# A decoder layer on one core: two of a summed pair's four weight sums made by accumulating DMAs, and three summed pairs per gate/up block in place of two

## The chip, the cores and the metric

The kernel runs on one core of a Trainium2 chip. The metric is the time of one execution on the device, in microseconds. The kernel before was timed three times: 1112.45, 1113.87 and 1114.35 us, median 1113.87 us. One more execution was profiled; it took 1112.63 us, and the trace below is of that one.

## The reference, cut to what matters

One layer of a hybrid decoder, for 256 tokens of width 2048, all in float32: a combined input projection, an RG-LRU branch and a retention branch, an output projection, and then the feed-forward part, which the change is about:

```
u  = rmsnorm(h, ln2_w)
ff = silu(u @ w_ffn_gate) * (u @ w_ffn_up)     # both weights (2048, 5632)
h  = h + ff @ w_ffn_down                       # weight (5632, 2048)
out = rmsnorm(h, final_norm_w)
```

Every weight is used once, so all of them come from DRAM during the run (the trace shows 211.67 MB read).

## The kernel before, in words

**Split products.** A float32 operand x is split into a high part h, rounded to the format that TensorE multiplies fast, and the remainder l = x - h. `split` (L100) does it: a cast on ScalarE (L101, the tiles `wh`, `bh`, `ah`), then a subtraction on VectorE (L102, the tiles `wl`, `bl`, `al`). A product of two such operands is three matmuls: high by high (L658), high by low of the weight (L659) and low by high (L660). All weights pass through this split while TensorE works, so ScalarE and VectorE have one cast and one subtraction for every 512 KB of weights.

**Feed-forward blocks.** The gate/up part has 11 blocks (`ffn_block`, L674), the down part 2 (`down_block`, L747). A block walks over pairs of 128-row slices of the contraction, 8 pairs in a gate/up block and 22 in a down block. A pair's weights are 1 MB, four pieces of 128 x 512, in the order b11, b12, b22, b21 along a row; the activations are likewise four pieces a11, a12, a21, a22 (class `Left`, L515). A plain pair is the 2 by 2 block product with eight products (`EIGHT`, L627), so 24 matmuls, and adds to four accumulators c11, c12, c21, c22. A **summed pair** uses seven products (`SEVEN`, L631), so 21 matmuls, of sums of pieces, and adds to the four c and to p1, p5, p6, p7, which are folded in after the last summed pair of the block. Its weight sums are

```
t1 = b11 + b12    t2 = t1 + b22    t3 = b12 + b22    t4 = t2 + b21
```

Before, pairs 2 and 4 of each gate/up block are summed (`SUMMED`, L32), and pairs 2, 6, 10, 14, 18 of each down block (`SUMMED_DOWN`, L33): 22 + 10 = 32 summed pairs. In this text S2 is the summed pair 2 of a block, Q3 the plain pair 3.

**Loading.** `Quad.load` (L603) is called for each half (512 KB) of a pair, three halves ahead of the pair that is computed (`AHEAD`, L933). A half goes by one DMA on SyncE's queue (SP) to a tile `raw` of 128 x 1024. There are five such tiles (`rpool`, L44), which the sum tiles also use, and four each of `wh` and `wl` (`wpool`, L45). For a plain pair each half is cut (split) where it lies, and its `raw` tile is free after the subtraction L102. For a summed pair b11 is split by itself into two activation tiles; when the second half is there, VectorE makes t1, t2 (into the tile `ta`) and t3, t4 (into `tb`), at L619, L620, L622, L623, and three cuts follow: (t1, t2), (t3, t4), (b22, b21). So a summed pair has 3.5 casts and 3.5 subtractions of 128 x 1024, a plain one 2 of each.

**Order.** The kernel is written step by step, and a scheduler then orders the instructions of each engine; each engine and each DMA queue takes its own in that order. PSUM has four banks `mm` (p1, p5, p6, p7, and the transposes `ft`, `ht` and `rms`) and four banks `aux` for c11 to c22. When a block's accumulators are done, VectorE adds them up (L720, L722), which frees their banks for the next block, ScalarE and VectorE make the gated result (L696 to L698), and TensorE transposes it (`turn`, L700) one and two steps later.

Of the kernel before, what the change touches and what calls it, by code (L numbers as in the profile page):

```python
# [28 lines left out]

SUMMED = (2, 4)  # L32
SUMMED_DOWN = (2, 6, 10, 14, 18)  # L33


# [1 line left out]
def tile_hymba_layer(ctx: ExitStack, tc: tile.TileContext, A: dict, out: bass.AP):  # L37
# [62 lines left out]
    def split(dst_h, dst_l, src):  # L100
        act.copy(out=dst_h, in_=src)  # L101
        v.tensor_tensor(out=dst_l, in0=src, in1=dst_h.bitcast(F32), op=ALU.subtract)  # L102
# [116 lines left out]
    def defer(steps, f):  # L219
        later.append([steps, f])  # L220
# [368 lines left out]
    class Quad:  # L589
# [11 lines left out]
                self.parts[name] = h[:, n * 512 : n * 512 + 512], l[:, n * 512 : n * 512 + 512]  # L601

        def load(self, half):  # L603
            r = rpool.tile([P, 1024], F32, tag="raw", name=nm("raw"))
            nc.sync.dma_start(out=r, in_=self.src[:, half * 1024 : half * 1024 + 1024])
            if half == 0 and self.before:
                self.before()
            if not self.sums:
                self.cut(("b22", "b21") if half else ("b11", "b12"), r)
                return  # L610
            if half == 0:
                self.ra = r
                self.parts["b11"] = act_tile("bh", F32R), act_tile("bl", F32R)
                split(*self.parts["b11"], r[:, :512])
                return
# [3 lines left out]
            v.tensor_tensor(out=t1, in0=b11, in1=b12, op=ALU.add)  # L619
            v.tensor_tensor(out=t2, in0=t1, in1=b22, op=ALU.add)  # L620
            self.cut(("t1", "t2"), ta)
            v.tensor_tensor(out=t3, in0=b12, in1=b22, op=ALU.add)  # L622
            v.tensor_tensor(out=t4, in0=t2, in1=b21, op=ALU.add)  # L623
            self.cut(("t3", "t4"), tb)
            self.cut(("b22", "b21"), r)

# [46 lines left out]

    def ffn_block(j):  # L674
        def after(i):
            if j == 0 and i == SUMMED[-1] + 1:
                norm2()
            if j in (1, 2) and i < 2:
                resid_tok(2 * j - 2 + i)
            if j == NB - 1 and i == 0:  # L680
                load_fw()

        ps = {}
        quads = [Quad(A["w_gu"][j * (KT // 2) + i], i in SUMMED) for i in range(KT // 2)]
        block(quads, hh, ffn_post(j, ps), ps, after=after)

    def ffn_post(j, ps):
        part = {}

        def other(c, name, a, b, op=ALU.subtract):  # L690
            part[c] = act_tile(name)
            v.tensor_tensor(out=part[c], in0=a, in1=b, op=op)

        def gated(t):
            g, u, th = part["c21" if t else "c11"], part["c22" if t else "c12"], act_tile("th")
            act.activation(out=th, in_=g, func=AF.Tanh, scale=r2_half[:, t : t + 1])  # L696
            v.scalar_tensor_tensor(out=g, in0=th, scalar=1.0, in1=g, op0=ALU.add, op1=ALU.mult)
            v.scalar_tensor_tensor(out=g, in0=u, scalar=r2_sq[:, t : t + 1], in1=g, op0=ALU.mult, op1=ALU.mult)  # L698

        def turn(b):  # L700
            pt = bank("ft")
            for c in range(2):
                for t, g in enumerate((part["c11"], part["c21"])):
                    o = c * S + t * P
                    pe.transpose(pt[:, o : o + P], g[:, (2 * b + c) * P : (2 * b + c) * P + P], ident)  # L705
# [24 lines left out]
        return post  # L730

# [316 lines left out]
```

## Time and profile before

| | |
|---|---|
| median of three executions | 1113.87 us (1112.45 to 1114.35) |
| profiled execution | 1112.63 us |
| its span, first to last instruction | 1110.9 us |
| gate/up blocks in it | about 387 to 862 us |
| down blocks in it | about 862 to 1100 us |
| read from DRAM | 211.67 MB, 192 GB/s over the span |

PE is TensorE, PEld its weight loads, DVE VectorE, ACT ScalarE, POOL GpSimd, SP SyncE, whose queue (SPq) issues nearly all loads. A row of a list of waits says which engine, at which line, waited for whom: microseconds in all, times, the longest. A row of a tile's list gives the duration in ns (least, median, most); its last line the time from a DMA's issue to its landing. A row of the timeline begins with the start and the length in microseconds; in brackets stands how long the engine was idle before, and who ended that. A row of stretches gives the busy time of each engine, the granted clock of TensorE, the busy share of the 16 DMA engines, and GB/s.

### The profile page before, as it was taken

Reading aid. Unit: us, or ns where it says so; the run is one execution under the profiler, and the core shown is the slowest. Engines: PE = TensorE matmul, PEld = TensorE weight load, DVE = VectorE, ACT = ScalarE, POOL = GpSimd, SP = SyncE. Lnnn points to the kernel's source line nnn. Section 1 sums busy time; section 2 is a strip of 40 time slices with the busy share of each in tenths; the row PEclk is TensorE's granted clock in tenths of the full one; section 3 lists DMA queues with packets and bytes.
Section 4 is the critical chain, followed back from the end, with each engine's and each line's share of the span. In section 5 each row is a group of like instructions: output and inputs, shape, how many; then the busy total and the mean of one; then the engine's idle time right before and its main releaser. Section 6 shows DMA issues by size and latency. Waiting matters only on the chain.

```text
span 1110.9 us, 15099 instructions
## 1 busy us (share of the span) xinstructions
PE 1096.1 (99%) x5584; PEld 934.2 (84%) x5584; DVE 878.0 (79%) x1229; ACT 617.3 (56%) x826; POOL 58.1 (5%) x64
## 2 busy tenths in 40 slices
PE   9999999999999999999999999999999999999995
PEld 7998888889988988888888888888888888888884
DVE  7797799978766787788778877877887988886665
ACT  7666644468465665554554555545546665554453
POOL 0602230000000000000000000000000000020001
PEclk9999999999999999999999999999999999999998
DMA  9764575554665555645746646656556456655662
GB/s 329 236 198 151 174 252 167 169 188 146 201 198 187 171 192 183 212 147 186 239 138 219 226 152 227 193 186 228 170 187 229 171 176 198 233 186 193 192 220 80
DMA packets 62218, 214.74 MB, mean 193 GB/s; under 512 B 7105, under 2 KB 7489, under 8 KB 62145
## 3 DMA queue, kind: packets, MB, share of 16 engines
q1 hardware_dynamic: 61344, 211.70, 57.8%
q0 software_dynamic: 512, 1.57, 0.4%
q8 instruction: 43, 0.70, 0.3%
q10 hardware_dynamic: 288, 0.52, 0.1%
q14 instruction: 31, 0.25, 0.1%
HBM read 211.67 MB, written 2.10 MB: 192 GB/s over the span
## 4 chain that ended last, share of the span: by engine, by line
PE 97%; ACT 1%; POOL 1%; DVE 0%; DMA 0%; issue 0%; SPq 0%; DVEq 0%; POOLq 0%
PE c L658 18%; PE c L659 18%; PE c L660 18%; PE fm L140 10%; PE fm L141 5%; PE fm L146 3%; PE fm L147 3%; PE fm L145 3%; PE p L660 3%; PE p L658 3%; PE p L659 3%; PE tm L156 3%; PE tm L157 3%; PE tm L158 3%; PE ft L705 1%; POOL sumsq L289 1%
## 5 line engine op out<-in xcount | busy, mean ns | idle before, releaser
L102 DVE TENSOR_TENSOR wl<-raw,wh 128x1024 fp32r<-128x1024 f32 (+1 forms) x368 | 440.7, 1209 | 151.2 <-ACT wh L101 149.4
L101 ACT CAST wh<-raw 128x1024 fp32r<-128x1024 f32 (+1 forms) x368 | 375.8, 1032 | 297.3 <-PE c L660 145.1
L659 PE MATMUL c<-wl,ah 128*128 128x512 f32 x864 | 333.1, 391 | 0.0
L660 PE MATMUL c<-wh,al 128*128 128x512 f32 x864 | 331.8, 389 | 0.0
L658 PE MATMUL c<-wh,ah 128*128 128x512 f32 x864 | 292.1, 389 | 0.0
L659 PEld LDWEIGHTS c<-wl,ah 128*128 128x128 f32 x864 | 162.2, 188 | 33.5 <-DVE wl L102 0.4
L658 PEld LDWEIGHTS c<-wh,ah 128*128 128x128 f32 x864 | 162.1, 188 | 33.4
L660 PEld LDWEIGHTS c<-wh,al 128*128 128x128 f32 x864 | 162.3, 188 | 33.0
L101 ACT CAST wh<-sum 128x1024 fp32r<-128x1024 f32 x64 | 66.8, 1054 | 81.3 <-PE c L660 52.7
L140 PE MATMUL fm<-u,wh 128*128 128x512 f32 x256 | 90.7, 398 | 0.0
L140 PE MATMUL fm<-y,wh 128*128 128x512 f32 x224 | 78.9, 398 | 0.0
L102 DVE TENSOR_TENSOR wl<-sum,wh 128x1024 fp32r<-128x1024 f32 x64 | 76.7, 1217 | 2.2 <-ACT wh L101 1.6
L146 PE MATMUL fm<-u,wh 128*128 128x256 f32 x256 | 72.7, 284 | 0.0
L145 PE MATMUL fm<-u,wh 128*128 128x256 f32 x256 | 72.7, 284 | 0.0
L147 PE MATMUL fm<-u,wl 128*128 128x256 f32 x256 | 72.3, 283 | 0.0
L141 PE MATMUL fm<-u,wl 128*128 128x256 f32 x256 | 71.9, 281 | 0.0
L141 PE MATMUL fm<-y,wl 128*128 128x256 f32 x224 | 62.4, 281 | 0.0
L807 POOL TENSOR_TENSOR htok<-htok,fw 128x512 f32<-128x512 f32 (+1 forms) x7 | 10.5, 1509 | 914.0 <-ACT junk L805 914.0
L140 PEld LDWEIGHTS fm<-u,wh 128*128 128x128 f32 x256 | 48.1, 188 | 11.7
L619 DVE TENSOR_TENSOR sum<-raw 128x512 f32<-128x512 f32 x32 | 22.0, 687 | 37.9 <-DMA raw<-in_w_down 23.0
L140 PEld LDWEIGHTS fm<-y,wh 128*128 128x128 f32 x224 | 41.9, 188 | 10.2
L146 PEld LDWEIGHTS fm<-u,wh 128*128 128x128 f32 x256 | 49.1, 192 | 0.1
(242 smaller groups left out, 1489.5 us busy)
## 6 DMA issues: line engine op xcount, KB each, us to landing
raw<-in_w_gu SPq DMA_DIRECT2D x176, 512.0 KB, 5.0
raw<-in_w_down SPq DMA_DIRECT2D x88, 512.0 KB, 5.1
raw<-in_w_out SPq DMA_DIRECT2D x32, 512.0 KB, 4.2
raw<-in_w_lx SPq DMA_DIRECT2D x16, 512.0 KB, 4.9
raw<-in_w_k SPq DMA_DIRECT2D x16, 512.0 KB, 3.7
raw<-in_w_q SPq DMA_DIRECT2D x16, 512.0 KB, 4.2
raw<-in_w_rg SPq DMA_DIRECT2D x16, 512.0 KB, 3.7
raw<-in_w_lg SPq DMA_DIRECT2D x16, 512.0 KB, 3.8
```

Of the source, the lines that this page charges most:

```text
L101: act.copy(out=dst_h, in_=src)
L102: v.tensor_tensor(out=dst_l, in0=src, in1=dst_h.bitcast(F32), op=ALU.subtract)
L140: pe.matmul(ps, wh, hl, start=first, stop=False)
L141: pe.matmul(ps[:, :S], wl, hl[:, :S], start=False, stop=last)
L145: pe.matmul(ps, wh, hl[:, :S], start=first, stop=False)
L146: pe.matmul(ps, wh, hl[:, S:], start=False, stop=False)
L147: pe.matmul(ps, wl, hl[:, :S], start=False, stop=last)
L156: pe.matmul(ps, ah, wh, start=first, stop=False)
L157: pe.matmul(ps, ah, wl, start=False, stop=False)
L658: pe.matmul(p, ah, bh, start=firsts[c] == m, stop=False)
L659: pe.matmul(p, ah, bl, start=False, stop=False)
L660: pe.matmul(p, al, bh, start=False, stop=last)
```

## The change

Three things change. `SUMMED` becomes (1, 3, 5): three summed pairs in each gate/up block, 33 + 10 = 43 in all. A summed pair is loaded in another way: b12 is loaded twice, to the first halves of `ta` and `tb`, b11 once to an activation tile of its own, all three on SP's queue; then two DMAs on GpSimd's queue read b11 and b22 from DRAM again and add them to what lies in `ta` and `tb`, which makes t1 and t3 there. b22 and b21 come as before in one load, and VectorE makes only t2 and t4. Each accumulating DMA waits for the landing of the b12 under it. And both transposes of a block's result come one step after it (the second came two steps after), and `norm2` one step earlier with respect to the last summed pair.

```diff
-SUMMED = (2, 4)
+SUMMED = (1, 3, 5)
...
+        def load_summed(self, half):
+            b11, b12, b22 = (self.src[:, n * 512 : n * 512 + 512] for n in range(3))
+            if half == 0:
+                self.ta, self.tb = (rpool.tile([P, 1024], F32, tag="raw", name=nm("sum")) for _ in range(2))
+                t1, t3 = self.ta[:, :512], self.tb[:, :512]
+                nc.sync.dma_start(out=t1, in_=b12)
+                nc.sync.dma_start(out=t3, in_=b12)
+                r = act_tile("b11")
+                nc.sync.dma_start(out=r, in_=b11)
+                pool.dma_start(out=t1, in_=b11, accum_op=ALU.add)
+                pool.dma_start(out=t3, in_=b22, accum_op=ALU.add)
+                if self.before:
+                    self.before()
+                self.parts["b11"] = act_tile("bh", F32R), act_tile("bl", F32R)
+                split(*self.parts["b11"], r)
                 return
-            b11, b12, b22, b21 = self.ra[:, :512], self.ra[:, 512:], r[:, :512], r[:, 512:]
-            ta, tb = (rpool.tile([P, 1024], F32, tag="raw", name=nm("sum")) for _ in range(2))
-            t1, t2, t3, t4 = ta[:, :512], ta[:, 512:], tb[:, :512], tb[:, 512:]
-            v.tensor_tensor(out=t1, in0=b11, in1=b12, op=ALU.add)
-            v.tensor_tensor(out=t2, in0=t1, in1=b22, op=ALU.add)
+            ta, tb = self.ta, self.tb
+            r = rpool.tile([P, 1024], F32, tag="raw", name=nm("raw"))
+            nc.sync.dma_start(out=r, in_=self.src[:, 1024:2048])
+            v.tensor_tensor(out=ta[:, 512:], in0=ta[:, :512], in1=r[:, :512], op=ALU.add)
             self.cut(("t1", "t2"), ta)
-            v.tensor_tensor(out=t3, in0=b12, in1=b22, op=ALU.add)
-            v.tensor_tensor(out=t4, in0=t2, in1=b21, op=ALU.add)
+            v.tensor_tensor(out=tb[:, 512:], in0=ta[:, 512:], in1=r[:, 512:], op=ALU.add)
             self.cut(("t3", "t4"), tb)
             self.cut(("b22", "b21"), r)
...
-            if j == 0 and i == SUMMED[-1] + 1:
+            if j == 0 and i == SUMMED[-1]:
                 norm2()
...
-                defer(3, lambda: turn(1))
+                defer(2, lambda: turn(1))
```

**Where it moves instructions, on SP and POOL.** The loads of one summed pair of a gate/up block in SP's queue, and the plain loads behind them. Before, in the fifth block (numbers are those of the tiles; 1122 and 1131 are the halves of S2, 1140 and 1145 those of Q3):

```order
L605 DMA raw_1122_5829<-in_w_gu 128x1024
L605 DMA raw_1131_5870<-in_w_gu 128x1024
L605 DMA raw_1140_5890<-in_w_gu 128x1024
L605 DMA raw_1145_5927<-in_w_gu 128x1024
L605 DMA raw_1148_5933<-in_w_gu 128x1024
```

After, S1 (`sum_1141` is its ta, `sum_1142` its tb, `raw_1148` its b22 and b21), Q2, and the first loads of S3:

```order
L619 DMA sum_1141_5858<-in_w_gu 128x512
L622 DMA b11_1143_5862<-in_w_gu 128x512
L620 DMA sum_1142_5859<-in_w_gu 128x512
L632 DMA raw_1148_5906<-in_w_gu 128x1024
L608 DMA raw_1155_5922<-in_w_gu 128x1024
L608 DMA raw_1166_5970<-in_w_gu 128x1024
L619 DMA sum_1169_5976<-in_w_gu 128x512
L620 DMA sum_1170_5977<-in_w_gu 128x512
L632 DMA raw_1178_6013<-in_w_gu 128x1024
```

and in POOL's queue, which holds nothing else in the gate/up part:

```order
L623 DMA sum_1141_5858<-in_w_gu 128x512
L624 DMA sum_1142_5859<-in_w_gu 128x512
L623 DMA sum_1169_5976<-in_w_gu 128x512
L624 DMA sum_1170_5977<-in_w_gu 128x512
L623 DMA sum_1191_6065<-in_w_gu 128x512
```

Two loads of 512 KB become four loads on SP and two on POOL. A tile's buffer comes from one that was freed earlier: `sum_1141` takes that of the second half of Q6 of the block before, `sum_1142` and `raw_1148` those of the halves of Q7, `sum_1169` and `sum_1170` (S3) those of `sum_1141` and `sum_1142`, and S5's (`sum_1191`, `sum_1192`) those of S3's; Q7's halves take those of S5's.

**On VectorE at a block's end.** The additions that free the banks c11 and c21 (L720 and L722; L732 and L734 after) and the sums of the first summed pair of the next block. Before:

```order
L720 TENSOR_TENSOR c11_1094_5675<-c11_1046_5481,c11_1094_5675 128x512
L722 TENSOR_TENSOR c21_1097_5690<-c21_1047_5488,c21_1097_5690 128x512
L619 TENSOR_TENSOR sum_1132_5872<-raw_1122_5829 128x512
L720 TENSOR_TENSOR c12_1096_5688<-c12_1048_5495,c12_1096_5688 128x512
L697 SCALAR_TENSOR_TENSOR c11_1094_5675<-th_1117_5808,c11_1094_5675 128x512
L620 TENSOR_TENSOR sum_1132_5872<-sum_1132_5872,raw_1131_5870 128x512
```

After:

```order
L633 TENSOR_TENSOR sum_1141_5858<-sum_1141_5858,raw_1148_5906 128x512
L732 TENSOR_TENSOR c11_1127_5788<-c11_1073_5557,c11_1127_5788 128x512
L635 TENSOR_TENSOR sum_1142_5859<-sum_1141_5858,raw_1148_5906 128x512
L734 TENSOR_TENSOR c21_1130_5803<-c21_1074_5564,c21_1130_5803 128x512
L732 TENSOR_TENSOR c12_1129_5801<-c12_1075_5571,c12_1129_5801 128x512
```

The sums t2 and t4 of the next block's S1 now stand ahead of the additions that free c11 and c21.

**On TensorE, where a block's first summed pair begins.** After, the end of Q0's 24 matmuls and what follows (before, 24 matmuls of the plain pair Q1 stand between Q0 and S2):

```order
L672 MATMUL c22_1161_5949<-wh_1139_5854,al_635_3519 128x512
L670 MATMUL c21_1159_5935<-wh_1151_5914,ah_655_3629 128x512
L717 MATMUL ft_1162_5956<-ident_91,c11_1127_5788 128x128
L717 MATMUL ft_1164_5963<-ident_91,c11_1127_5788 128x128
L670 MATMUL p1_1174_5988<-bh_1144_5866,ah_655_3629 128x512
```

`wh_1151` is the cast of `sum_1142`, S1's (t3, t4). It is the first thing of S1 that TensorE wants, 24 matmuls after the last of the block before.

More of the change, by code (lines that the diff above doesn't have):

```diff
@@ L603, in load @@
         def load(self, half):
+            if self.sums:
+                self.load_summed(half)
+                return
             r = rpool.tile([P, 1024], F32, tag="raw", name=nm("raw"))
@@ L607, in load @@
                 self.before()
-            if not self.sums:
-                self.cut(("b22", "b21") if half else ("b11", "b12"), r)
-                return
[L611 to L615, printed above, removed]
-            b11, b12, b22, b21 = self.ra[:, :512], self.ra[:, 512:], r[:, :512], r[:, 512:]
-            ta, tb = (rpool.tile([P, 1024], F32, tag="raw", name=nm("sum")) for _ in range(2))
-            t1, t2, t3, t4 = ta[:, :512], ta[:, 512:], tb[:, :512], tb[:, 512:]
-            v.tensor_tensor(out=t1, in0=b11, in1=b12, op=ALU.add)
-            v.tensor_tensor(out=t2, in0=t1, in1=b22, op=ALU.add)
+            self.cut(("b22", "b21") if half else ("b11", "b12"), r)
+        def load_summed(self, half):
[13 more added lines that the diff above has]
+                split(*self.parts["b11"], r)
+                return
+            ta, tb = self.ta, self.tb
+            r = rpool.tile([P, 1024], F32, tag="raw", name=nm("raw"))
+            nc.sync.dma_start(out=r, in_=self.src[:, 1024:2048])
+            v.tensor_tensor(out=ta[:, 512:], in0=ta[:, :512], in1=r[:, :512], op=ALU.add)
             self.cut(("t1", "t2"), ta)
-            v.tensor_tensor(out=t3, in0=b12, in1=b22, op=ALU.add)
-            v.tensor_tensor(out=t4, in0=t2, in1=b21, op=ALU.add)
+            v.tensor_tensor(out=tb[:, 512:], in0=ta[:, 512:], in1=r[:, 512:], op=ALU.add)
             self.cut(("t3", "t4"), tb)
```

## The prediction

> **What bounds the kernel now.** I read the page first: the busy shares and the chain that ended last.
>
> ```profile
> span 1110.9 us, 15099 instructions
> PE 1096.1 (99%) x5584; PEld 934.2 (84%) x5584; DVE 878.0 (79%) x1229; ACT 617.3 (56%) x826; POOL 58.1 (5%) x64
> ...
> PE 97%; ACT 1%; POOL 1%; DVE 0%; DMA 0%; issue 0%; SPq 0%; DVEq 0%; POOLq 0%
> ```
>
> TensorE is the chain: 97%. A busy PE need not be a full one, so next the stretches of a steady part of the gate/up blocks, and who waits there:
>
> ```profile
> core 0: us, PE busy (x) PEld busy (x) DVE busy (x) ACT busy (x) POOL busy (x), PEclk, DMA share, GB/s
> 596.00:638.00 42.00, 42.00 (x191) 34.72 (x190) 33.95 (x40) 21.45 (x25) 0.00 (x0) 1.00 0.60 197
> ```
> ```profile
> ACT wh L101 <- PE c L660: 197.8, 121, 3.8
> DVE sum L619 <- DMA raw<-in_w_gu: 14.8, 9, 2.5
> ```
> ```profile
> SPq L605 <- DVE wl L102: 421.4, 218, 9.5
> ```
> ```profile
> L659 PEld LDWEIGHTS c<-wl,ah 128*128 128x128 f32 x864 | 162.2, 188 | 33.5 <-DVE wl L102 0.4
> ```
>
> The clock is 1.00, and over the whole run TensorE's second matmul of a product waited 0.4 us for its `wl`. The casts wait for TensorE (197.8 us, 121 times): the split runs ahead until `wh` is full. SP waits 421.4 us for a subtraction to free a `raw` tile: loads start when a buffer comes free, not when there is bandwidth. The DMAs are 0.60 busy. But the lead is not large everywhere. In the timeline of the fifth block, ScalarE and then TensorE, behind S4:
>
> ```profile
> 588.49 1.05 ACT L101 CAST wh<-raw 128x1024 fp32r<-128x1024 f32 x1 [1.46 <-DMA raw<-in_w_gu]
> ```
> ```profile
> 559.88 0.39 PE L658 MATMUL c<-wh,ah 128*128 128x512 f32 x1
> ...
> 566.45 0.39 PE L660 MATMUL c<-wh,al 128*128 128x512 f32 x1
> ...
> 590.76 0.39 PE L658 MATMUL c<-wh,ah 128*128 128x512 f32 x1
> ```
>
> The cast of Q5's second half waited for its DMA and ended at 589.54; TensorE took it at 590.76. So the smallest lead is 1.2 us, just behind a summed pair, where five `raw` tiles are shortest.
>
> **Matmuls.** From 559.88 to 566.45 stand 30 matmuls, 29 steps: 6.57 / 29 = 0.2266 us each. The third summed pair takes 3 matmuls from each of 11 blocks: 33 x 0.2266 = 7.48 us, all on the chain. A block goes from 194 instructions (186 matmuls, 8 transposes) to 191. This term is sure; all else is whether anything now makes TensorE wait.
>
> **VectorE and ScalarE.** Their durations:
>
> ```profile
> L101 ACT CAST wh<-sum 128x1024 fp32r<-128x1024 f32 x64 | 66.8, 1054 | 81.3 <-PE c L660 52.7 <-DVE sum L623 18.8 <-DVE sum L620 5.9
> L102 DVE TENSOR_TENSOR wl<-sum,wh 128x1024 fp32r<-128x1024 f32 x64 | 76.7, 1217 | 2.2 <-ACT wh L101 1.6
> L622 DVE TENSOR_TENSOR sum<-raw,raw 128x512 f32<-128x512 f32 x32 | 22.9, 717 | 0.6 <-DMA raw<-in_w_down 0.6
> L623 DVE TENSOR_TENSOR sum<-sum,raw 128x512 f32<-128x512 f32 x32 | 22.9, 716 | 0.0
> L619 DVE TENSOR_TENSOR sum<-raw 128x512 f32<-128x512 f32 x32 | 22.0, 687 | 37.9 <-DMA raw<-in_w_down 23.0 <-DMA raw<-in_w_gu 14.8
> L620 DVE TENSOR_TENSOR sum<-sum,raw 128x512 f32<-128x512 f32 x32 | 21.9, 684 | 1.3 <-DMA raw<-in_w_down 0.6 <-DMA raw<-in_w_gu 0.5
> ```
>
> Four sums cost 2.80 us, the two that stay 1.40. Per block the sums go from 5.6 to 4.2 us, and the third summed pair adds 1.5 subtractions, 1.83 us: together +0.4 us on 34.0 busy of 42. ScalarE gets 1.5 casts more, 1.6 us on 21.5. Neither becomes the bound; cost nothing, covered by the 8 us that VectorE idles in such a stretch. S1's activation sums (four small subtractions and a split, once, in the output projection), the earlier transposes and the earlier `norm2` I put at zero, between nothing and one us together.
>
> **Traffic.** A summed pair reads 1.75 MB, not 1: a gate/up block 5 x 1 + 3 x 1.75 = 10.25 MB, not 8. The share goes from 0.60 to about 0.60 x 10.25 / 8 x 194 / 191 = 0.78, if an adding DMA costs the engines as much as a plain one. If it costs twice (it also reads its destination), 1.5 MB more: 0.89.
>
> **Two landings in series.** No accumulating DMA is in the trace. The nearest rows: plain loads of 512 KB in a steady block, DMAs on POOL's queue (192 KB, eight in a row), and loads of x (256 KB and two of 128), then the write of the result.
>
> ```profile
> L605 SPq DMA_DIRECT2D raw<-in_w_gu x15: 327/328/328, 700.9 to 741.0; - x15
> ...
> DMA to landing us min/median/max: 3.1/5.2/6.1
> ```
> ```profile
> L414 POOL DMA_DIRECT2D decay<-in_decay x8: 536/536/732, 142.7 to 146.6; - x8
> ...
> DMA to landing us min/median/max: 3.5/5.9/6.2
> ```
> ```profile
> L848 SPq DMA_DIRECT2D x<-in_x x7: 327/328/432, 3.5 to 15.4; - x7
> ...
> DMA to landing us min/median/max: 3.4/5.4/5.8
> ```
>
> The b12 load (256 KB) I take at 3.5 us, bounds 3.1 to 5.4. The accumulation I take at 4.5, bounds 3.5 to 6.2: nearer the least, because the median row stands behind up to seven of its kind and an accumulation behind one. POOL's queue issues one in 0.54 us and has nothing else to hold up. A chain is then 8.0 us (6.6 to 11.6) where a plain load has 5.2.
>
> The Trainium skill's page "DMA: Bandwidth & Descriptors", section "Anatomy of one DMA", gives 2.0 us plus bytes / 436 GB/s for a DMA issued from GpSimd; my estimate from it is 2.6 us for 256 KB. By that a chain is 5.2 us, nothing below is tight, and the time is the forecast's lower end. The trace's POOL row is longer (3.5 us at the least, for 192 KB).
>
> The walk through a steady block needs three more rows. On TensorE, with transposes between matmuls:
>
> ```profile
> 573.75 0.39 PE L660 MATMUL c<-wh,al 128*128 128x512 f32 x1
> 573.98 0.49 PE L705 MATMUL ft<-ident,c 128*128 128x128 f32 x3
> ...
> 574.54 0.39 PE L660 MATMUL c<-wh,al 128*128 128x512 f32 x1
> ```
>
> Between the starts lie three transposes and two steps of matmuls: (0.79 - 0.45) / 3 = 0.11 us a transpose. And the end of a block, VectorE and TensorE:
>
> ```profile
> 591.91 2.35 DVE L102 TENSOR_TENSOR wl<-raw,wh 128x1024 fp32r<-128x1024 f32 x2
> ...
> 594.77 2.58 DVE L102 TENSOR_TENSOR wl<-raw,wh 128x1024 fp32r<-128x1024 f32 x2
> ```
> ```profile
> 605.50 0.39 PE L660 MATMUL c<-wh,al 128*128 128x512 f32 x1
> ```
>
> Q7 ends with that matmul, at 605.7; call it T. The subtractions of Q6's second half and Q7's two end at 594.3, 596.0 and 597.35, so the three buffers that S1 of the next block takes come free at T-11.4, T-9.6 and T-8.3. In the changed order the cast of S3's (t1, t2) stands 72 matmuls and 8 transposes behind T, T+17.2; S5's 117 and 8, T+27.4; the next block begins at T+42.4.
>
> - S1: ta is summed by T-3.4, b22 and b21 land by T-3.1: in time. The casts wait for Q7's last matmuls; VectorE ends (t1, t2) at about T+2.0 and (t3, t4), behind the additions and gatings of the old block, at T+4.4, wanted from T+5.4. Lead 1 us or more.
> - S3: its ta takes a buffer free at T+2.0, summed at T+10.1. Its b22, b21 tile waits for S1's third cut (T+6.9) and lands 5.2 later, T+12.1. Sum 0.7, cast 1.05, subtraction 1.22, with a plain cut between: T+15.5, wanted from T+17.2. Lead near 2 us.
> - S5: its ta's buffer is free at T+15.5, issue behind three loads at 16.0, summed at 24.0; its raw tile, free at 18.4, lands at 23.6. The cast ends at T+26.2, wanted at 27.4; the subtraction, behind t4 on VectorE, at T+27.4, wanted two matmuls later, at 27.9. Lead 0.5 us. (t3, t4) ends 1.2 later, wanted at 29.2.
> - Q7's second half takes the buffer of S5's (t3, t4): lands T+33.8, cut by T+36.1. That buffer is the next S1's b22, b21: lands T+41.3, then t2 and the addition that frees c11's bank, 1.4 us: T+42.7, wanted T+42.4. Lead -0.3 us.
>
> So with these values every chain just closes: 0.3 us a block is missing, 3 us in all at most; I take 1, as a block that begins late gives the loads behind it as much more time. In the down blocks a summed pair stands between three plain ones; its buffers come free as S1's do, with no old block's additions in the way, and the 10 pairs there cost nothing and gain nothing.
>
> Sum: 1112.63 - 7.5 + 1 (leads) + 0 = 1106.1 us for the profiled execution, whose span of 1110.9 leaves 1.7 us around it that the change does not touch. It lies 1.24 us under the median, so the forecast is **1107.4 us**.
>
> **The rivals.**
> 1. *Slower: the accumulation lands late, and the buffers go round too slowly.* It decides from the S5 step: beyond 5.0 us the lead of 0.5 is gone, and each further us delays (t1, t2) of S5 by one; the same late buffer carries Q7 and the next S1. At 6.0 us: 1.0 late at S5, about 0.7 more at the block's end: 1.7 x 11 = 19 us, 1113.87 - 7.5 + 19 = 1125 us. It breaks even at 7.5 / 11 = 0.68 us a block, an accumulation of about 5.2 us (0.2 at S5, 0.5 at the block's end). For it: the 5.9 of the POOL row, and loads that land at 5.2 where DMAs queue. Against: the 3.5 of the same row. Chance 0.33.
> 2. *No change: loads slower by the traffic.* With the share at 0.78 a plain load lands nearer the row's 6.1 than its 5.2. That comes straight onto the next S1's raw tile, where t2 stands ahead of the addition that frees c11: 0.3 + 0.4 us a block, 11 x 0.7 = 7.7: 1114 us. Chance 0.13.
> 3. *Slower by much: the DMA engines are full between S1 and S5.* 197 GB/s at 0.60 is 328 GB/s in full. From T+5.4 to T+31.6 TensorE uses three summed pairs and two plain, 7.25 MB, which takes 23.2 us. With accumulations at double cost it is 8.75 MB (9.18 million bytes), 28.0 us, 1.8 too long; with landings at the row's upper end as in rival 1, 3.5 us a block: 38 us, 1145 us. A window of the before shows both queues busy together:
>
> ```profile
> q0 software_dynamic: 512, 1.57, 44.9%
> q1 hardware_dynamic: 456, 1.65, 40.0%
> ```
>
> These are the 11 us of the decay loads; 85% busy, and there they landed at 5.9. The page named above says in "Issuing engines are not separate DMA queues" that DMAs of all issuers run on the same 16 engines and interleave; that window agrees. Against: Q6, Q7, Q0 need only 3 MB in 16 us, and give some back. Chance 0.09.
>
> **How the numbers follow.** The forecast has 0.45: the term of 7.5 us is sure, and the middle values close, but just. Its own range is 1105 (no lead lost, 1113.87 - 7.5 = 1106.4, less a us of scatter) to 1111. A measurement of this kernel can tell about 0.2%, 2.2 us, from no change; faster means below 1111.6. Faster 0.45, same 0.13, slower 0.42. The range for 8 in 10 goes from 1105 to 1130: it takes in rivals 1 and 2 and leaves out rival 3 and the tail of 1.
>
> **What would show it.** Right: 5551 matmuls and transposes in place of 5584, gate/up stretches of 42 us still 42.00 busy with x191 or so, PEld rows that wait under 1 us for DVE or ACT, accumulations landing below 5 us. S5's cast or subtraction as releaser of TensorE, or c11's addition, with microseconds per block, shows rival 1 or 2; a DMA share near 0.9 shows 3. An accumulation that lands above 5.2 us while TensorE still never waits would prove my walk wrong: then leads exist that I do not see.

## The result and the profile after

The changed kernel takes 1236.31 us, median of four executions (1234.56 to 1249.69); the kernel before, run beside it, 1113.16 us. The ratio is 1.113, 95% interval 1.108 to 1.119: slower by 123 us, where 1107.4 was forecast. The profiled execution took 1236.18 us. Its page, first the rows that answer to those shown of before:

```profile
span 1234.4 us, 15511 instructions
PE 1132.9 (92%) x5551; PEld 944.0 (76%) x5551; DVE 880.0 (71%) x1214; ACT 628.9 (51%) x849; POOL 131.2 (11%) x150
...
PE 36%; DMA 34%; DVE 15%; issue 8%; ACT 6%; POOL 1%; SPq 0%; ACTq 0%; POOLq 0%; DVEq 0%
```

The 33 matmuls are gone (5584 to 5551), but TensorE is no longer the chain: a third of it is DMA. The difference of the spans, 1234.4 - 1110.9 = 123.5 us, has three parts. TensorE idles 1234.4 - 1132.9 = 101.5 us where it idled 14.8: +86.7. The missing matmuls: -7.5. And 5551 instructions at the old rate would be busy 1096.1 - 7.5 = 1088.6 us; they were busy 1132.9: +44.3 for the same work. What TensorE waits for, and the landings of the accumulating DMAs (t1 at L623, t3 at L624; least, median, most):

```profile
PE c L670 <- DVE c L732: 37.1, 10, 4.7
PE p L670 <- ACT wh L101: 27.3, 16, 3.2
PE c L671 <- DVE wl L102: 15.6, 16, 2.3
```
```profile
L623 POOL DMA_DIRECT2D sum<-in_w_gu x33: 864/873/924, 376.5 to 940.8; - x33
...
DMA to landing us min/median/max: 3.6/6.2/8.7
```
```profile
DMA to landing us min/median/max: 3.7/7.5/10.0
```

c11's addition is the largest wait, the sums' casts and subtractions follow. The next rows show what such a wait costs. They are TensorE at the start of a block, in the timeline and as stretches (the last three columns are the granted clock, the DMA share and GB/s):

```profile
540.96 0.39 PE L672 MATMUL c<-wh,al 128*128 128x512 f32 x1
545.13 0.76 PE L670 MATMUL c<-wh,ah 128*128 128x512 f32 x1 [3.78 <-DVE c L732]
545.70 0.63 PE L671 MATMUL c<-wl,ah 128*128 128x512 f32 x1
...
549.53 0.63 PE L671 MATMUL c<-wl,ah 128*128 128x512 f32 x1
...
550.35 0.39 PE L670 MATMUL c<-wh,ah 128*128 128x512 f32 x1
550.58 0.40 PE L671 MATMUL c<-wl,ah 128*128 128x512 f32 x1
```
```profile
541.00:545.10 4.10, 0.35 (x2) 0.00 (x0) 3.14 (x5) 1.12 (x2) 0.00 (x0) 0.80 0.77 200
545.10:549.00 3.90, 3.87 (x9) 3.12 (x10) 3.90 (x6) 2.20 (x3) 0.00 (x0) 0.50 0.31 121
549.00:553.00 4.00, 4.00 (x16) 3.20 (x16) 2.58 (x4) 0.34 (x1) 0.87 (x1) 0.84 0.38 128
```

After a wait of 3.8 us the granted clock is 0.50: nine steps between 545.70 and 549.53 take 3.83 us, 0.43 each in place of 0.23, until 550.35. Twelve matmuls are slow, so the wait costs 3.8 us and then some 2.5 more. The Trainium skill's page "TensorE: Matmul & The Clock Gate", section "Part 1: The HAM clock gate", says that TensorE drops to half rate after an idle window of about 3.4 us and needs about as much sustained work to come back; this trace shows the half rate (for 5.2 us here), but not that a wait must be that long. Later in the same block a wait of 1.4 us is followed by full steps:

```profile
577.65 0.73 PE L670 MATMUL p<-wh,sh 128*128 128x512 f32 x2 [1.44 <-ACT wh L101]
578.91 0.50 PE L671 MATMUL p<-wl,sh 128*128 128x512 f32 x1 [0.52 <-DVE wl L102]
579.25 0.40 PE L672 MATMUL p<-wh,sl 128*128 128x512 f32 x1
```

A wait of 3.24 us that ends at 705.54 is followed by full steps as well, and one of 2.17 us that ends at 844.02 by slow ones. In this trace the granted clock goes down only at points that are 3.41 us, or a multiple of it, apart. Cut there, the stretches around the 3.24 us and those around the 2.17 us look like this:

```profile
700.48:703.89 3.41, 1.82 (x9) 1.17 (x7) 0.51 (x1) 0.00 (x0) 0.00 (x0) 1.00 1.08 306
703.89:707.30 3.41, 1.76 (x8) 1.50 (x9) 3.38 (x7) 1.87 (x3) 0.00 (x0) 1.00 0.28 96
840.42:843.84 3.42, 1.43 (x7) 0.85 (x5) 1.39 (x2) 0.92 (x1) 0.00 (x0) 1.00 0.82 240
843.84:847.25 3.41, 2.73 (x6) 1.73 (x7) 2.56 (x3) 2.74 (x5) 0.00 (x0) 0.50 0.27 93
```

The longer wait falls into two stretches, in each of which TensorE is just over half busy, and the clock stays; the shorter one leaves one stretch 0.42 busy, and the clock falls behind it. All 15 drops from 380 us on, the last one behind the end of the work left out, fall behind a stretch that was at most 0.49 busy; the stretches at full clock that no drop follows were at least 0.48 busy.

**The loop.** Where the 10 us a block come from is seen when the three ta of one block are followed: SP's loads of b12 into ta, GpSimd's accumulating DMAs, then VectorE's sum t2 and the subtraction that frees ta.

```profile
531.38 0.33 SPq L619 DMA_DIRECT2D sum<-in_w_gu  x1
...
547.94 0.33 SPq L619 DMA_DIRECT2D sum<-in_w_gu  x1
...
555.00 0.33 SPq L632 DMA_DIRECT2D raw<-in_w_gu  x1
...
564.33 0.33 SPq L619 DMA_DIRECT2D sum<-in_w_gu  x1
...
584.70 0.33 SPq L619 DMA_DIRECT2D sum<-in_w_gu  x1
```
```profile
537.07 0.87 POOL L623 DMA_DIRECT2D sum<-in_w_gu  x1 [19.91 <-DMA sum<-in_w_gu]
...
551.45 0.87 POOL L623 DMA_DIRECT2D sum<-in_w_gu  x1 [12.08 <-DVE c L710]
...
568.53 0.87 POOL L623 DMA_DIRECT2D sum<-in_w_gu  x1 [14.42 <-DVE wl L102]
```
```profile
541.96 0.69 DVE L633 TENSOR_TENSOR sum<-sum,raw 128x512 f32<-128x512 f32 x1 [1.93 <-DMA sum<-in_w_gu]
...
546.70 1.21 DVE L102 TENSOR_TENSOR wl<-sum,wh 128x1024 fp32r<-128x1024 f32 x1
...
560.61 0.69 DVE L633 TENSOR_TENSOR sum<-sum,raw 128x512 f32<-128x512 f32 x1 [4.50 <-DMA raw<-in_w_gu]
...
563.08 1.22 DVE L102 TENSOR_TENSOR wl<-sum,wh 128x1024 fp32r<-128x1024 f32 x1
...
575.70 0.69 DVE L633 TENSOR_TENSOR sum<-sum,raw 128x512 f32<-128x512 f32 x1 [5.66 <-DMA sum<-in_w_gu]
...
577.63 1.22 DVE L102 TENSOR_TENSOR wl<-sum,wh 128x1024 fp32r<-128x1024 f32 x1 [0.52 <-ACT wh L101]
```

S1's b12 is issued at 531.38, its accumulation at 537.07, t2 waits for it until 541.96, and the subtraction ends at 547.91. At 547.94, as that buffer comes free, S3's b12 is issued; its link ends at 564.30, and at 564.33 S5's b12 is issued; that link ends at 578.85. The next S1's b12 follows at 584.70, when Q6's second half is cut. The links are 16.6, 16.4 and 14.5 us and the rest 5.9: 53.3 us, the period of the block. TensorE needs 42.4 for it. S1's and S5's links run over their accumulating DMAs (4.9 and 7.1 us from issue to landing). In S3's link the accumulation had landed by about 555, and it is the b22, b21 tile that comes last: issued only at 555.00, when S1's third cut freed its buffer. That cut was late because of TensorE, as far as the trace shows it:

```profile
552.19 0.39 PE L672 MATMUL c<-wh,al 128*128 128x512 f32 x1
```
```profile
552.66 1.05 ACT L101 CAST wh<-raw 128x1024 fp32r<-128x1024 f32 x1 [5.36 <-issue]
```

The cast of the third cut starts 0.08 us behind the end of the 21st matmul since the wait, the last that reads the first half of Q0, whose `wh` tile is by the order the next of the four to be used again. The trace names no releaser for this cast, so that is read from the order and the times alone. By it the late start of the block, and the clock behind it, go on into S3's load.

### The profile page after: what moved, and what is told of

Read it like the earlier page. It is cut to its first block, busy times and chain, and to the rows that moved or that the text cites. A ratio compares the mean times of both kernels' runs of the same rounds, so it can differ in the third digit from the quotient of the medians.

```text
span 1234.4 us, 15511 instructions
## 1 busy us (share of the span) xinstructions
PE 1132.9 (92%) x5551; PEld 944.0 (76%) x5551; DVE 880.0 (71%) x1214; ACT 628.9 (51%) x849; POOL 131.2 (11%) x150
## 3 DMA queue, kind: packets, MB, share of 16 engines
q0 software_dynamic: 12896, 24.12, 11.4%
## 4 chain that ended last, share of the span: by engine, by line
PE 36%; DMA 34%; DVE 15%; issue 8%; ACT 6%; POOL 1%; SPq 0%; ACTq 0%; POOLq 0%; DVEq 0%
DMA sum<-in_w_gu 17%; PE fm L140 9%; DVE wl L102 9%; DMA sum<-in_w_down 7%; PE fm L141 5%; DMA raw<-in_w_gu 4%; ACT wh L101 4%; DMA b<-in_w_gu 3%; PE fm L146 2%; PE fm L147 2%; PE c L671 2%; PE fm L145 2%; PE c L670 2%; PE c L672 2%; PE tm L156 2%
## 5 line engine op out<-in xcount | busy, mean ns | idle before, releaser
L102 DVE TENSOR_TENSOR wl<-raw,wh 128x1024 fp32r<-128x1024 f32 (+1 forms) x357 | 427.3, 1211 | 95.3 <-ACT wh L101 94.2
L101 ACT CAST wh<-raw 128x1024 fp32r<-128x1024 f32 (+1 forms) x357 | 361.7, 1030 | 236.9 <-PE c L672 63.4
L672 PE MATMUL c<-wh,al 128*128 128x512 f32 x798 | 316.9, 399 | 0.0
L101 ACT CAST wh<-sum 128x1024 fp32r<-128x1024 f32 x86 | 89.5, 1045 | 172.0 <-DVE sum L633 129.0
L633 DVE TENSOR_TENSOR sum<-sum,raw 128x512 f32<-128x512 f32 x43 | 30.8, 716 | 174.0 <-DMA sum<-in_w_gu 82.6
L102 DVE TENSOR_TENSOR wl<-sum,wh 128x1024 fp32r<-128x1024 f32 x86 | 104.5, 1220 | 26.1 <-ACT wh L101 25.6
L623 POOL DMA_DIRECT2D sum<-in_w_gu x33 | 28.9, 875 | 671.7 <-DMA sum<-in_w_gu 355.4
L670 PE MATMUL p<-wh,sh 128*128 128x512 f32 x129 | 46.9, 414 | 27.3 <-ACT wh L101 27.3
L671 PE MATMUL p<-wl,sh 128*128 128x512 f32 x129 | 54.3, 421 | 3.3 <-DVE wl L102 3.2
L140 PEld LDWEIGHTS fm<-u,wh 128*128 128x128 f32 x256 | 48.1, 188 | 11.7
```

The costliest lines, as they stand in the source:

```text
L140: pe.matmul(ps, wh, hl, start=first, stop=False)
L623: pool.dma_start(out=t1, in_=b11, accum_op=ALU.add)
L633: v.tensor_tensor(out=ta[:, 512:], in0=ta[:, :512], in1=r[:, :512], op=ALU.add)
L670: pe.matmul(p, ah, bh, start=firsts[c] == m, stop=False)
L671: pe.matmul(p, ah, bl, start=False, stop=False)
L672: pe.matmul(p, al, bh, start=False, stop=last)
```

## The experiments

All times, with the median of the kernel before at 1113.1 to 1113.2 in every comparison. "Ten blocks" is the time from the first to the last gating activation (ScalarE on `th`, 428.7 to 865.0 before: 436.3), "down" from there to the last start of a TensorE product of summed pieces (`p` from `wh` and `sh`), both from the profiled execution (those of half and sums2_x6 were 9 and 7 us above the medians). Thirty matmuls fewer would make ten blocks 6.8 us shorter.

| kernel | us | ratio (95%) | ten blocks | down |
|---|---|---|---|---|
| before | 1113.2 | | 436.3 | 214.2 |
| changed | 1236.3 | 1.108 to 1.119 | 528.8 | 234.2 |
| third | 1123.7 | 1.008 to 1.011 | 441.6 | 214.1 |
| sums2 | 1146.7 | 1.026 to 1.034 | 448.4 | 233.5 |
| plain | 1179.9 | 1.057 to 1.063 | 489.5 | 220.2 |
| noacc | 1115.5 | 1.001 to 1.003 | 436.6 | 214.4 |
| apart | 1172.3 | 1.052 to 1.055 | 435.3 | 213.8 |
| apart2 | 1139.0 | 1.022 to 1.025 | 455.9 | 215.9 |
| behind | 1227.4 | 1.100 to 1.104 | 524.6 | 233.7 |
| third_behind | 1134.3 | 1.017 to 1.021 | 456.6 | 215.3 |
| s246 | 1261.3 | 1.128 to 1.142 | 554.2 | 234.8 |
| third246 | 1131.0 | 1.016 to 1.018 | 448.8 | 212.5 |
| after_x6 | 1227.1 | 1.096 to 1.106 | 542.0 | 214.4 |
| third_x6 | 1125.9 | 1.010 to 1.013 | 439.5 | 216.2 |
| sums2_x6 | 1138.8 | 1.020 to 1.028 | 464.2 | 215.8 |
| raw6 | 1210.9 | 1.087 to 1.090 | 507.9 | 229.1 |
| s3own | 1218.2 | 1.093 to 1.097 | 518.2 | 228.6 |
| half | 1226.6 | 1.100 to 1.107 | 531.6 | 228.2 |
| half_own2 | 1152.5 | 1.033 to 1.039 | 468.2 | 213.1 |
| own2 | 1160.8 | 1.037 to 1.045 | 478.2 | 216.0 |

**Each part alone: third and sums2.** The kernel before with the third summed pair, and the changed kernel with two.

```diff
-SUMMED = (2, 4)
+SUMMED = (1, 3, 5)
```
(third: in the kernel before, with the changed times of `norm2` and of the transposes; sums2: the other way round in the changed kernel.)

> Gate/up pairs 1, 3, 5 summed, all weight sums by VectorE as before; nothing is added by a DMA. Theory A (an adding DMA behind the landing of b12 makes the sums late, and TensorE then waits and loses clock): without adding DMAs nothing is late, the 33 matmuls are the whole change: 1113.2 - 7.5 = 1105.7, between 1104 and 1108 us. Theory B (the third summed pair itself is too much for five raw tiles, however the sums are made): 1150 us or more. Theory C (the DMA engines are full, because the sums are read twice and an adding byte costs double): the traffic is that of before, 1106 us as by A.

> Two of four weight sums by adding DMAs, but with pairs 2 and 4 of a gate/up block summed as before. Theory A: two chains of two landings a block instead of three, and the first one's sums no longer in front of the additions that free the block's first bank; what is left is about half of the loss in the gate/up blocks (102 us between the gated results of the first and last block) and all of the 20 us in the down blocks: 1160 to 1190 us. Theory B: the third pair's part goes, the down blocks stay: 1113 + 20 = 1133 us or less. Theory C: two thirds of the added traffic: 1113 + 20 + 0.6 x 102 = about 1195 us.

The third pair alone makes the kernel 10.6 us slower, not 7.5 faster: 18 us are lost. None of the theories had that. TensorE waits there 11.7 us for the addition that frees c11:

```profile
PE c L658 <- DVE c L720: 11.7, 9, 2.4
```

The accumulating DMAs with two pairs cost 33.5 us, 12 in ten blocks and 19 in the down part; that is less than A's 47 and more than B's 20. Together that is 44 of the 123 us, so most of the loss comes only when three pairs and accumulating DMAs meet.

**The two DMAs left out, or without the adding: noacc and plain.**

```diff
-                pool.dma_start(out=t1, in_=b11, accum_op=ALU.add)
-                pool.dma_start(out=t3, in_=b22, accum_op=ALU.add)
```
(noacc: t1 and t3 stay b12. plain keeps both lines without `accum_op`, so that b11 and b22 are written over b12. Both leave the two additions out.)

> As the changed kernel without the two DMAs on GpSimd's queue (t1 and t3 stay b12; both additions are left out). Everything else stands: three summed pairs, loads of 256 KB, buffers, order. Theory A: one landing, then nothing is late: 1106 us, at most 1112. Theory B: 1190 us or more. Theory C: 8.75 MB a block in place of 10.25, about 1106 us as well.

> As the changed kernel, but the two DMAs on GpSimd's queue do not add: they write b11 and b22 over b12, so t1 and t3 are left out. Same bytes, same wait for the landing below, same buffers. Theory A: the second landing is still there but should be some 4.5 us and not 7.2; with three such landings in the loop of a block some 6 to 8 us a block come back: 1150 to 1175 us. Theory B: the time of the changed kernel, 1236 us. Theory C: adding at double cost gone, the DMA engines busy 0.78 and not full: 1106 to 1120 us.

Without the two DMAs the loss is gone but for 2.3 us, and 9.8 us of the gain stay out: the third pair costs that much even then. Theory B as the main cause falls. With DMAs that only write, in series, 64 us come on top (a little over A's range, far from C's), and the adding adds 56 more. Plain's landings in the places of L623 and L624:

```profile
DMA to landing us min/median/max: 3.2/4.3/7.1
```
```profile
DMA to landing us min/median/max: 3.0/5.6/7.7
```

Adding lands 1.9 us later in both medians (6.2 and 7.5). Three links of 1.9 us in ten blocks would be 57 us; the ten blocks are 39 us longer than plain's and the down part 14. So not every link pays its 1.9 us, which fits the S3 link above.

**Bytes or series: apart and apart2.** The DMAs add into tiles that nobody reads.

```diff
-                pool.dma_start(out=t1, in_=b11, accum_op=ALU.add)
-                pool.dma_start(out=t3, in_=b22, accum_op=ALU.add)
+                for d, t, b in zip(dump, (t1, t3), (b11, b22)):
+                    pool.tensor_copy(out=d[:, 0:1], in_=t[:, 0:1])
+                    pool.dma_start(out=d, in_=b, accum_op=ALU.add)
```
(apart2; in apart the copy was missing.)

> The changed kernel with its two adding DMAs per summed pair adding into two tiles of their own that nobody reads (t1 and t3 stay b12, both additions are left out; two tiles fewer for activations). Same number and kind of DMAs, same bytes, but nothing waits for them. Theory A (the series of two landings): about the 1115.5 us that the kernel without these DMAs took, at most 1125. Theory C (an adding byte costs the DMA engines double and slows all other loads): 1160 us or more.

> A second try at adding DMAs that nobody waits for: they add into two tiles of their own, in the room of a tile that is not used, and each is held back by a copy of one column of its b12 on GpSimd, so that it starts when b12 has landed, as in the changed kernel (t1 and t3 stay b12: both additions are left out). Theory A (the series of two landings is the loss): the 1115.5 us of the kernel without these DMAs, at most 1122. Theory C (adding bytes fill the DMA engines and slow the other loads): 1160 us or more, with the plain loads landing well above 5 us.

apart tells nothing of the question: with nothing to wait for, the DMAs were all ordered into the first 300 us, where they cost 57 us, and the gate/up part had none. In apart2 they run where they belong. Its time lies between what A (at most 1122 us) and C (1160 or more) expected: 23.5 us more than noacc, 19 of them in the ten blocks; the DMA engines are 0.80 busy there, more than in the changed kernel, and TensorE does 1508 instructions in 360 us:

```profile
500.00:860.00 360.00, 343.81 (x1508) 276.50 (x1507) 278.42 (x314) 185.50 (x213) 76.79 (x95) 0.99 0.80 234
```
```profile
500.00:860.00 360.00, 315.30 (x1310) 249.90 (x1309) 240.03 (x268) 162.19 (x187) 35.83 (x41) 0.94 0.71 205
```

The first row is apart2, the second the changed kernel: 0.71, 1310. So the bytes cost something (theory C, 24 us; the copies, which hold ta a little longer, are in that), but the large loss comes with fewer bytes per us. It is the waiting for them.

**The order at the block's start: behind, third_behind, s246, third246.**

```diff
-            v.tensor_tensor(out=ta[:, 512:], in0=ta[:, :512], in1=r[:, :512], op=ALU.add)
+            with behind():
+                v.tensor_tensor(out=ta[:, 512:], in0=ta[:, :512], in1=r[:, :512], op=ALU.add)
```
(behind: what stands under it is queued on VectorE after the addition that frees c21; third_behind does it for t1 and t3 of the kernel third, with t3 ahead of t2. s246 and third246: `SUMMED = (2, 4, 6)` in the changed kernel and in third.)

> The changed kernel, with one order changed: on VectorE the first sum of a block's first summed pair (t2 of S1) is put behind the additions that free c11 and c21 of the block before. Theory A1 (the order at the block's start is the main cost: t2 waits for the adding DMA, and the addition that frees c11 stands behind it): the 37.1 us that TensorE waited for that addition go, and the clock that it lost after each of the ten waits (the granted clock was 0.81, 0.50 and 0.84 in the twelve us from the wait on, some 2.5 us of matmuls each): 1236 - 37 - 25 = about 1175 us. Theory A2 (the five raw tiles go round no faster than four landings in series allow, some 53 us a block): TensorE only waits elsewhere, 1220 to 1236 us.

> Three summed pairs with all sums by VectorE (1123.7 us before this edit, where TensorE waited 11.7 us for the addition that frees c11), and the first summed pair's first sums put behind the additions that free c11 and c21. Theory A1: the 11.7 us and the clock lost behind them go: 1106 us. Theory A2 (the third pair makes the loads late whatever the order): 1118 to 1124 us.

> The changed kernel with pairs 2, 4, 6 of a gate/up block summed in place of 1, 3, 5: the first one's sums come a plain pair later, behind the additions that free the banks, and the spacing within a block is the same. Theory A1: as with the order put right, about 1175 us. Theory A2: the time of the changed kernel, 1220 to 1240 us.

> Pairs 2, 4, 6 summed and all sums by VectorE. With 1, 3, 5 it took 1123.7 us where the matmuls alone give 1105.7. If the first summed pair next to the block's start is the cause (its sums meet the additions and gatings of the old block on VectorE), 2, 4, 6 gives 1106 to 1110 us. If the load on VectorE and the tiles is the cause wherever the pairs stand: 1120 us or more.

A1, my first reading of the wait for c11, falls. With the order put right that wait sinks to 7.5 us, but TensorE waits as much for the casts and subtractions:

```profile
PE p L677 <- ACT wh L107: 27.2, 18, 4.4
PE c L678 <- DVE wl L108: 26.6, 14, 3.2
...
PE c L677 <- DVE c L739: 7.5, 7, 2.3
```

Only 9 us come back. The third pair alone became slower by it (1134.3, above both ranges), and pairs 2, 4, 6 are worse in both kernels: s246 lies above both of its ranges too, third246 in that of the load on VectorE and the tiles. Why these are slower is open.

**More tiles: after_x6, third_x6, sums2_x6, raw6, s3own.** A sixth weight tile, in the room of a tile that the last norm does not use; it serves all ta (the three x6), or S3's ta only (s3own); raw6 has it in the pool, with two activation tiles fewer.

```diff
-                self.ta, self.tb = (rpool.tile([P, 1024], F32, tag="raw", name=nm("sum")) for _ in range(2))
+                self.ta, self.tb = ta_tile(), rpool.tile([P, 1024], F32, tag="raw", name=nm("sum"))
```

> The changed kernel with a sixth tile for weights in the feed-forward part: ta has a buffer of its own (in the room of a tile that is not used), so S3's ta waits for S1's and no plain load waits for a ta. Theory A2 (buffers that come free late, and landings in series behind them): one of the four landings in the loop of a block goes, 5 to 8 us a block: 1236 - 55 to 90 = 1146 to 1180 us. Theory C (full DMA engines): 1225 to 1236 us.

> Three summed pairs with all sums by VectorE, and the same sixth tile for ta. Theory A2: the third pair's own loss (1123.7 us measured, 1105.7 by the matmuls) comes from too few tiles, so most of it goes: 1106 to 1111 us. Its rival (VectorE's order and load, 313 us busy of 360 there): 1120 to 1124 us, no matter how many tiles.

> Two summed pairs a block, with two of four sums by adding DMAs (1146.7 us with five tiles), and the sixth tile for ta. Theory A2: the tile takes away most of the wait: 1113 to 1125 us. Theory C: the traffic is the same, so 1140 to 1147 us.

> The changed kernel with six weight tiles in one pool in place of five (two tiles fewer for activations). Theory A2, put as a sum of tile times: a summed pair's ta and tb are held some 16 us each and its raw tile 10, ten plain halves 8.5 each, so a block wants 3 x 42 + 85 = 211 us of tile time and has 5 x 42.4 = 212; with six it has 254, and the waits in the gate/up blocks go down by more than half: 1236 to 1150 - 1185 us. Its rival (the chain of landings S1, S3, S5, each b12 issued when the cut of the summed pair before frees its buffer, about 17 us a link, whatever the number of tiles): 1215 to 1236 us.

> The changed kernel with a sixth tile in the feed-forward part that only S3's ta uses (in the down blocks every other summed pair), so that S3's b12 and the adding DMA behind it do not wait for S1's cut. Theory A2 as a chain of links: the chain S1, S3, S5 is cut in the middle, ta's part of the waits goes: 1150 to 1190 us. As a sum of tile times alone: about 1160 to 1190. Theory C: 1225 to 1236 us.

None did what A2 expected as a lack of tiles. From the changed kernel 9 us (after_x6), 18 (s3own) and 25 (raw6) came back, from sums2 8, and third_x6 is 2 us slower than third. In after_x6 the 20 us of the down part vanish (214.4), as in sums2_x6, but ten blocks become longer: all three ta of a block now share one buffer, so S3's b12 waits for S1's cut as before. raw6 has six tiles as well and does the reverse: its ten blocks are shorter (507.9), and its down part keeps most of the loss (229.1). So the theory falls by which only the number of tiles counts (the sum of tile times in raw6's expectation). In third_x6 a tile for ta does nothing for the third pair's own loss.

**The links: half, half_own2, own2.** In half only t1 is made by an accumulating DMA; half_own2 and own2 give S3's and S5's ta each a tile of its own.

```diff
-                pool.dma_start(out=t3, in_=b22, accum_op=ALU.add)
...
+            v.tensor_tensor(out=tb[:, :512], in0=tb[:, :512], in1=r[:, :512], op=ALU.add)
```
(half; half_own2 has in addition `own=i in SUMMED[1:]`, by which ta comes from a pool of two tiles.)

> Of the two adding DMAs only the one for t1 stays; t3 is made by VectorE from b12, which lies in tb as before, and b22. Theory A2: ta's chain is as long as before (b12 then an adding DMA), tb's is one landing; the adding DMA stands alone and lands sooner than the 6.2 us median of the first one: less than half of the loss stays, 1140 to 1175 us. Theory C: half of the 24 us that adding bytes cost with nobody waiting goes: 1224 us.

> One adding DMA per summed pair, for t1 alone (1226.6 us with five tiles, the DMA engines 0.60 busy), and S3's and S5's ta each in a tile of its own in the feed-forward part (two tiles more in all, two fewer for activations), so that no ta waits for the cut of the summed pair before. Link theory (a block's period is three links of b12, adding DMA, sum and cuts, 16 to 17 us each, plus the 69 matmuls behind S5, less the lead of the next S1): the links of S3 and S5 are gone, what stays is S1, whose adding DMA lands at the block's end: 1110 to 1150 us. Rival (something else in these DMAs makes loads and sums late): above 1190 us.

> The same two tiles of their own for S3's and S5's ta, with both adding DMAs as in the changed kernel. Link theory: the links of tb stay (S1's, S3's and S5's tb still go round in the five tiles, b12 and an adding DMA that lands in 7.5 us): most of the loss stays, 1180 to 1215 us, well above the kernel with one adding DMA. Rival (ta's links were all, since t3 is wanted later than t1): like the kernel with one adding DMA, within 20 us.

One accumulating DMA does nearly the damage of two, at the DMA share that the kernel before has. A2's range for half was missed by 50 us, since the single DMA landed no sooner (6.3 us in the median); theory C's 1224, which takes away 12 us for half of the added bytes, was met:

```profile
500.00:860.00 360.00, 316.14 (x1313) 252.79 (x1311) 249.54 (x288) 161.93 (x186) 17.39 (x21) 0.93 0.60 188
```

Half of the added bytes gave back 10 us, and the DMA engines are no busier than before the change: the main loss is not bandwidth. The same links show in GpSimd's queue of half, one block and the next S1 (starts 16.7, 15.5 and 22.0 us apart, together 54.2):

```profile
591.24 0.87 POOL L623 DMA_DIRECT2D sum<-in_w_gu  x1 [20.82 <-DMA b<-in_w_gu]
607.90 0.86 POOL L623 DMA_DIRECT2D sum<-in_w_gu  x1 [15.79 <-DVE c L710]
623.44 0.87 POOL L623 DMA_DIRECT2D sum<-in_w_gu  x1 [14.68 <-DMA sum<-in_w_gu]
645.42 0.86 POOL L623 DMA_DIRECT2D sum<-in_w_gu  x1 [21.12 <-DMA b<-in_w_gu]
```

With S3's and S5's ta taken out of the chain 74 us come back (1226.6 to 1152.5): just over the link theory's range, and well under its rival's. (Between the profiled executions it is 87 us, 63 of them in ten blocks and 15 in the down part.) From the changed kernel to own2, which keeps both accumulating DMAs, the same two tiles bring 75. One tile brought 9 to 25, depending on whom it served. But these are two tiles more, and two more in the common pool were not tried; so it is not shown how much of the 75 us is due to their place and how much to their number. own2, where tb still has its links, is only 8 us slower. There the theory was wrong on tb: its links, which I expected to keep 1180 us or more, hardly count, and ta's were nearly all. What TensorE still waits for in half_own2 is c11's addition, behind S1's t2, whose link begins at Q6's cut; the clock behind these waits comes on top (0.984 over the span):

```profile
PE c L677 <- DVE c L739: 27.4, 10, 3.3
```

No kernel here beats the one before. half_own2 together with the order of behind was not tried.

## Why the prediction was wrong

**The matmuls.** 33 fewer, 7.5 us: right, and the only term that was.

**The walk.** Its mechanism was there: ta holds a buffer through two landings, S3's follows S1's, S5's follows S3's, and the next block's S1 follows. But the step failed that said a block that begins late gives the loads behind it as much more time. It does not: the next loads wait for buffers that the late sums hold, and where they wait for TensorE, as S3's b22, b21 tile seems to in the block shown, the late block makes them later still. Read as a loop, the walk had links of 13.4 (T-11.4 to T+2.0), 13.5 and 11.9 us and a rest of 3.6 to the next block, together 42.4; its own leads say how little was to spare (0.5 us at S5, -0.3 at the block's end). Measured, in the one block followed, were 16.6, 16.4, 14.5 and 5.9: each 2 to 3 us more, 10.9 in all, and nothing gives them back. Half of S1's excess is its b12 (5.2 in place of 3.5 us), S5's is the accumulation (7.1 in place of 4.5), S3's the late third cut. half_own2 and own2 bear the loop out: with ta's waits at S3 and S5 taken away, some 75 us of the loss are gone (with what is said there of the number of tiles).

**The landing of the accumulation.** I took 4.5 us, bounds 3.5 to 6.2. The medians were 6.2 and 7.5, so the second was beyond the upper bound. The argument for the lower end (one of its kind stands behind it, not seven) failed: what lands beside it are loads of other queues, and with the DMA engines 0.60 busy, alone on its queue, half's single one still took 6.3 in the median. The landing of b12 (3.5 taken; 3.7 and 3.1 in the median) was right. The estimate of 2.6 us from the Trainium skill's page "DMA: Bandwidth & Descriptors", section "Anatomy of one DMA", by which the change would have been free, does not hold for a DMA that adds: 3.6 us at the least. The plain ones in plain took 3.0 at the least.

**Rival 1** was the case, from its point of 5.2 us on, with a price that was too small: 19 us for an accumulation of 6.0, worked out from lateness that the rest of the block absorbs. Rival 3 (full DMA engines) is not it: the share is 0.71 in the stretch above.

**The price of a wait.** I counted a microsecond of waiting as one. Of the 131 us by which the span exceeds the old one less the matmuls (86.7 + 44.3), some 30 are TensorE running slowly after its waits: an estimate from the granted clock over the span, 0.970 where it was 0.996, 0.026 x 1234 = 32. The other 12 or so of the 44.3 are not accounted for.

**S1's step.** "In time" was wrong: in the block shown ta was summed not at T-3.4 but 0.7 us behind T, since its b12 took 5.2 us there and the accumulation 4.9. So t2, which the diff put ahead of the addition that frees c11, held that up, as the prediction had it for the next S1's raw tile. But this wait was where the loop shows and not its cause: moved away, most of it came back elsewhere (behind).

**VectorE, at zero.** The third pair costs 18 us with VectorE's sums and 9.8 with none of the accumulations. VectorE is 313 of 360 us busy in third (286 before), and it is late with c11's addition. The stretches before and in third:

```profile
500.00:860.00 360.00, 360.00 (x1620) 297.67 (x1619) 286.04 (x333) 188.72 (x210) 0.00 (x0) 1.00 0.60 199
```
```profile
500.00:860.00 360.00, 348.98 (x1559) 286.66 (x1558) 313.26 (x374) 195.59 (x223) 0.00 (x0) 1.00 0.55 190
```

No edit took this away (order, other pairs, a sixth tile), so its cause stays open. The term was not zero.

**Traffic.** The doubled cost of an adding byte was rightly bounded. By apart2 the bytes alone cost some 24 us, where I had put zero in the sum and 0.89 as a bound of the share.

## What to carry to other kernels

A tile that is filled by two DMAs in series holds its buffer for both landings. Before such a change, write the buffers' rotation as a loop over one period and add up its links; if the sum is near the period of the engine that bounds the kernel, every late microsecond is paid in every period, and a wait that left TensorE under half busy in one of the clock's stretches of 3.41 us was paid again in clock. To test whether buffers' waits are the cause, give buffers of their own to all the tiles that the loop runs over, and the same number to the common pool beside it: here one more buffer brought 9 to 25 us, depending on whom it served, and two for the loop's tiles 75.

## What the runs showed of the hardware

An accumulating DMA takes the DMA engines about twice as long as a plain one. The shares of GpSimd's queue in the changed kernel, in plain and in noacc:

```profile
q0 software_dynamic: 12896, 24.12, 11.4%
```
```profile
q0 software_dynamic: 7392, 24.12, 6.5%
```
```profile
q0 software_dynamic: 512, 1.57, 0.4%
```

Less noacc's 0.4% of 1113.9 us, the 86 DMAs of 256 KB take 11.4% of 1234.4, (140.7 - 4.5) / 86 = 1.58 us of all 16 engines each, against (76.8 - 4.5) / 86 = 0.84 plain. They are sent as more packets, (12896 - 512) / 86 = 144 against 80. GpSimd is busy 0.87 us with the issue of one; the decay loads took 0.54.
